# A fused SwiGLU trunk: VectorE's low parts of weights in the order of use, both weight sums ahead of them, output blocks behind a unit's sums

## The chip, the cores and the metric

The kernel runs on one core of one Trainium2 chip. The metric is the device time of one execution in microseconds (us), of which the median of the runs is given. Matrix products run on TensorE (PE in the profile), which accumulates into PSUM banks of 128x512 float32. VectorE (DVE) and ScalarE (ACT) work on tiles of 128 partitions, GpSimd (POOL) and SyncE (SP) issue DMA transfers. Each engine works through its own queue in the order in which the instructions were put there, and waits at the head of the queue for what that instruction needs.

## The reference, cut to what matters

A trunk of two layers on 256 positions (two tiles of 128 rows) of width 2048, all in float32. Layer 0 has a gated mixer and layer 1 a sparse attention; the change touches neither. Behind each mixer come the feed-forward and a gated embedding:

```
D_MODEL, SEQ, PLE_DIM, FFN_DIM = 2048, 256, 256, 5632

def swiglu(h, w_in, w_out):
    g, u = jnp.split(h @ w_in, 2, axis=-1)
    return (jax.nn.silu(g) * u) @ w_out

def ple_add(x, p_i, norm_g, w_proj, w_gate):
    gate = jax.nn.sigmoid(rmsnorm(x, norm_g) @ w_gate)
    return x + (p_i @ w_proj) * gate

for i in range(DEPTH):
    x = x + mixer(rmsnorm(x, norm_mix[i]))
    x = x + swiglu(rmsnorm(x, norm_ffn[i]), ffn_w_in[i], ffn_w_out[i])
    x = ple_add(x, p[i], norm_ple[i], ple_w[i], ple_gate[i])
```

## The kernel before, in words

**Split products.** A float32 product is made of three matmuls in the format fp32r. Both factors are split into a high and a low part, and `mm3` (L155 to L157) sums high x high, high x low and low x high into one bank. The activations are split once. A weight block is split when it comes in (`split`, L148 and L149): ScalarE copies `raw` into the high part, rounding it, and VectorE subtracts that from `raw` for the low part. So each weight block asks for a load, a copy on ScalarE, a subtraction on VectorE and then its matmuls.

**Rings.** `wraw` loads a block of 128x2048 (1 MB) on SP's queue into one of three `raw` buffers, in the order of the blocks. A buffer can be loaded again when its last reader on ScalarE and VectorE is done. The pairs of high and low parts come from `wpair`: a ring of three (`wh` with `wl`), and from part 1 of the feed-forward on of four, in which the fourth lies in a tile called `w4` that holds both parts. A high part can be written again when TensorE has done the last matmul that reads it.

**A unit.** The first product of the feed-forward runs in 11 units `c` of 512 columns of `g` and 512 of `u` (`ffn_unit`, which calls `block_unit`). A unit has eight blocks, one for each two of the 16 tiles of the depth of 2048, and each holds four pieces of 128x512 weights. In an ordinary block all four pieces are used for both row tiles, 8 products of three matmuls. In a block of `pairs7` seven products do, in the manner of Strassen's and Winograd's: VectorE forms four sums of weight pieces in three operations, `t13` (L560, two pieces of 512 in one) and `t24` (L562, then L563, which reads the first half of `t24`):

```
nc.vector.tensor_tensor(t13, r[:, 1:3], r[:, 0:1].to_broadcast([P, 2, NC]), ALU.subtract)
nc.vector.tensor_tensor(t24[:, 0], r[:, 2], t13[:, 0], ALU.add)
nc.vector.tensor_tensor(t24[:, 1], r[:, 3], t24[:, 0], ALU.subtract)
```

The pieces of `raw` that are used as they are (1536 of 2048 columns) are split into one pair of high and low parts, then `t13` and `t24` (1024 columns each) into the halves of the next pair. So a block of seven products takes two pairs of the ring, and VectorE works for it in three sums and three low parts. Unit 0 has three such blocks of eight, units 1, 2 and 3 have four, five and six, and all later units six; the last block of each unit is an ordinary one. The products go into seven banks `p1` to `p7`. In the embedding stage two units of the gate product run through the same `block_unit` with three blocks of seven products each (`PLE_PAIRS`).

**The end of a unit.** `ffn_unit` puts the banks together. ScalarE copies `p1` (L598), VectorE adds `p6`, `p7`, `p2`, `p4`, `p5` and `p3` (`add` at L590, and L605), ScalarE takes two SiLUs (L602 and L604), and VectorE forms the products `up` (L606 and L608). TensorE transposes `up` (`mid_T`), ScalarE and VectorE split that into `aT0` or `aT1`.

**Output jobs.** The second product is cut into parts of one or two units, and each part into four jobs `out_job` of 512 output columns. Behind each unit two of the jobs of earlier parts run (banks `fo`, weight blocks from `in_ffn_w_out`, also through `wraw`, `wpair` and `split`). Each job's sums go to DRAM by a GpSimd DMA that accumulates (`xd<-part`). So between two units' blocks stand four output blocks of 128x2048 (two in the units where a part holds one unit).

**What sets the order.** The program text is not the order on the engines. A scheduler takes the next instruction for each engine among those whose inputs it expects to be ready. What is written under `issue_after(x)` is put behind `x` in the queue of `x`'s engine, without a semaphore; work on other engines isn't touched by it. Before the change none of the work of a unit has such an order, so the sums, low parts and copies stand where the scheduler put them. Layer 0's feed-forward runs from some 286 to 1025 us and layer 1's from some 1405 to 2110. In profile rows, `wl` and `w` (for `w4`) are weight parts, `t` the weight sums `t13` and `t24`, `p` a bank of a unit, `exh`, `exl`, `hF0h`, `hF1h` and the like the split activations.

Of the kernel before, what the change touches and what calls it, by code (L numbers as in the profile page):

```python
# [11 lines left out]
AF = mybir.ActivationFunctionType  # L12
ALU = mybir.AluOpType
# [83 lines left out]
def trunk_kernel(ctx: ExitStack, tc: tile.TileContext, a: dict, out: bass.AP):  # L97
# [40 lines left out]
    def gain(which, k):  # L138
        c = PK_GAIN + which * KD + k
        return pk[:, c:c + 1]  # L140

    def f32v(t):
        return t.bitcast(F32)

    def split(hi, lo, src, scale=None):

        if scale is None:
            nc.scalar.activation(hi, src, AF.Copy)  # L148
            nc.vector.tensor_tensor(lo, src, f32v(hi), ALU.subtract)  # L149
        else:  # L150
            nc.scalar.activation(hi, src, AF.Copy, scale=scale)
            nc.vector.scalar_tensor_tensor(lo, src, scale, f32v(hi), op0=ALU.mult, op1=ALU.subtract)

# [371 lines left out]
    def block_unit(c, forms, win, pairs, early=()):  # L525
# [22 lines left out]
        for at_, j in enumerate(order):  # L548
# [7 lines left out]
            if j in pairs7:  # L556
# [5 lines left out]
                nc.vector.tensor_tensor(t24[:, 0], r[:, 2], t13[:, 0], ALU.add)  # L562
                nc.vector.tensor_tensor(t24[:, 1], r[:, 3], t24[:, 0], ALU.subtract)  # L563
                split(wh[:, NC:], wl[:, NC:], raw[:, NC:])
                prod(1, j, plain(ka, 0), wh, wl, 1, j == last[1])
# [3 lines left out]
                for i, t in enumerate((t13, t24)):  # L569
                    split(wh[:, 2 * i * NC:2 * (i + 1) * NC], wl[:, 2 * i * NC:2 * (i + 1) * NC],  # L570
                          t.rearrange("p s n -> p (s n)"))
                prod(6, j, s2, wh, wl, 2, j == last[6])
# [3 lines left out]
            else:  # L576
                split(wh, wl, raw)
                for b, slots in ((2, (1, 3)), (4, (1, 3)), (5, (0, 2)), (3, (0, 2))):
# [10 lines left out]
    def add(o, p, i):  # L589
        nc.vector.tensor_tensor(o, p, i, ALU.add)  # L590

    def ffn_unit(c, forms, win, rstd, early=()):
# [6 lines left out]
        add(B[:, 0], bank[6], A[:, 0])  # L599
        add(B[:, 1], bank[7], B[:, 0])  # L600
        add(A[:, 0], bank[2], A[:, 0])
# [5 lines left out]
        add(B[:, 0], bank[3], B[:, 0])  # L607
        nc.vector.scalar_tensor_tensor(B[:, 0], B[:, 0], rs[:, 0:1], A[:, 0], op0=ALU.mult, op1=ALU.mult)  # L608
        return B
# [625 lines left out]
```

## Time and profile before

| | us |
|---|---|
| median of 3 runs (lowest, highest) | 2206.74 (2206.36, 2208.51) |
| the profiled execution | 2208.47 |
| its span on the core | 2206.8 |
| VectorE busy in low parts of 128x2048 and other sizes straight from `raw` (375 instructions) | 655.9 |
| VectorE busy in low parts of weight sums (202) | 243.3 |
| VectorE busy in the first weight sum, L560 (129) | 156.9 |
| ScalarE busy in the copies of `raw` (391) | 565.5 |

Read from it: VectorE's busy time holds mostly low parts and weight sums. The profile gives of a group of instructions the mean duration and the idle time of the engine ahead of them, with the engine that ended it. A matmul's row on the time line gives its start and how long it took from start to end; since matmuls overlap, the distance of two starts is what one costs. A row `x2` stands for two instructions.

### The profile page before, as it was taken

Reading aid. Unit: us, or ns where it says so; the run is one execution under the profiler, and the core shown is the slowest. Engines: PE = TensorE matmul, PEld = TensorE weight load, DVE = VectorE, ACT = ScalarE, POOL = GpSimd, SP = SyncE. Lnnn points to the kernel's source line nnn. Section 1 sums busy time; section 2 is a strip of 40 time slices with the busy share of each in tenths; the row PEclk is TensorE's granted clock in tenths of the full one; section 3 lists DMA queues with packets and bytes.
Section 4 is the critical chain, followed back from the end, with each engine's and each line's share of the span. In section 5 each row is a group of like instructions: output and inputs, shape, how many; then the busy total and the mean of one; then the engine's idle time right before and its main releaser. Section 6 shows DMA issues by size and latency. Waiting matters only on the chain.

```text
span 2206.8 us, 26808 instructions
## 1 busy us (share of the span) xinstructions
PE 2188.2 (99%) x10054; PEld 1814.3 (82%) x10054; DVE 1855.8 (84%) x2232; ACT 1351.2 (61%) x1694; POOL 78.3 (4%) x82
## 2 busy tenths in 40 slices
PE   8999999999999999999999999999999999999998
PEld 7888878878888888888888998888888888888887
DVE  5566679999999999878887888799999999999685
ACT  7555556656656565566677877556665565665563
POOL 0000000000000000000000000000000000000000
PEclk9999999999999999999999999999999999999999
DMA  8566555766666776764576455557667667666754
GB/s 314 190 194 228 194 201 191 226 229 224 207 209 218 229 228 210 254 208 171 177 257 201 139 168 194 178 201 238 204 199 234 224 219 234 219 221 211 247 177 153
DMA packets 132430, 464.68 MB, mean 211 GB/s; under 512 B 10811, under 2 KB 13243, under 8 KB 131884
## 3 DMA queue, kind: packets, MB, share of 16 engines
q1 hardware_dynamic: 117596, 431.14, 55.8%
q0 software_dynamic: 13264, 29.63, 7.2%
q10 hardware_dynamic: 1440, 2.20, 0.3%
q8 instruction: 79, 1.29, 0.2%
q14 instruction: 51, 0.42, 0.1%
HBM read 435.63 MB, written 28.38 MB: 210 GB/s over the span
## 4 chain that ended last, share of the span: by engine, by line
PE 89%; DVE 6%; ACT 2%; DMA 2%; issue 1%; SPq 0%; DVEq 0%; ACTq 0%
PE p L156 13%; PE p L157 13%; PE p L155 13%; PE fo L155 7%; PE fo L157 7%; PE fo L156 7%; DVE wl L149 2%; PE v L155 1%; PE v L156 1%; PE v L157 1%; PE ao L157 1%; PE bo L155 1%; PE bo L156 1%; PE bo L157 1%; PE ao L155 1%
## 5 line engine op out<-in xcount | busy, mean ns | idle before, releaser
L149 DVE TENSOR_TENSOR wl<-raw,wh 128x2048 fp32r<-128x2048 f32 (+3 forms) x375 | 655.9, 1753 | 178.0 <-ACT wh L148 177.5
L148 ACT ACTIVATE wh<-raw 128x2048 fp32r<-128x2048 f32 (+3 forms) x391 | 565.5, 1450 | 335.8 <-PE p L157 95.5
L148 ACT ACTIVATE wh<-t 128x1024 fp32r<-128x1024 f32 x202 | 211.8, 1059 | 163.7 <-DVE t L563 73.4
L149 DVE TENSOR_TENSOR wl<-t,wh 128x1024 fp32r<-128x1024 f32 x202 | 243.3, 1218 | 43.4 <-ACT wh L148 43.2
L156 PE MATMUL p<-wl,exh 128*128 128x512 f32 x443 | 174.1, 394 | 0.1
L157 PE MATMUL p<-wh,exl 128*128 128x512 f32 x443 | 172.7, 390 | 0.0
L155 PE MATMUL p<-wh,exh 128*128 128x512 f32 x443 | 168.4, 390 | 0.7 <-ACT wh L148 0.7
L560 DVE TENSOR_TENSOR t<-raw 128x1024 f32<-128x1024 f32 x129 | 156.9, 1216 | 2.4 <-DMA raw<-in_ple_gate 2.4
L156 PE MATMUL p<-wl,hF1h 128*128 128x512 f32 x310 | 121.2, 391 | 0.9 <-DVE wl L149 0.9
L148 ACT ACTIVATE w<-raw 128x1536 fp32r<-128x1536 f32 (+1 forms) x58 | 98.2, 1694 | 37.8 <-DMA raw<-in_ffn_w_in 15.3
L156 PE MATMUL p<-wl,hF0h 128*128 128x512 f32 x310 | 121.1, 391 | 0.3 <-DVE wl L149 0.3
L155 PE MATMUL p<-wh,hF0h 128*128 128x512 f32 x310 | 119.9, 390 | 0.4 <-ACT wh L148 0.4
L157 PE MATMUL p<-wh,hF0l 128*128 128x512 f32 x310 | 120.3, 390 | 0.0
L157 PE MATMUL p<-wh,hF1l 128*128 128x512 f32 x310 | 120.2, 390 | 0.0
L155 PE MATMUL p<-wh,hF1h 128*128 128x512 f32 x310 | 119.8, 390 | 0.0
L149 DVE TENSOR_TENSOR w<-raw,w 128x1536 fp32r<-128x1536 f32 (+1 forms) x58 | 116.4, 2007 | 0.6 <-ACT w L148 0.4
L155 PE MATMUL fo<-wh,aT0h 128*128 128x512 f32 x280 | 109.7, 392 | 0.3 <-DVE gt L590 0.3
L155 PE MATMUL fo<-wh,aT1h 128*128 128x512 f32 x280 | 109.7, 392 | 0.3 <-DVE gt L590 0.3
L157 PE MATMUL fo<-wh,aT0l 128*128 128x512 f32 x280 | 109.8, 392 | 0.0
L157 PE MATMUL fo<-wh,aT1l 128*128 128x512 f32 x280 | 109.8, 392 | 0.0
L156 PE MATMUL fo<-wl,aT0h 128*128 128x512 f32 x280 | 109.1, 389 | 0.0
L156 PE MATMUL fo<-wl,aT1h 128*128 128x512 f32 x280 | 109.0, 389 | 0.0
(345 smaller groups left out, 5129.0 us busy)
## 6 DMA issues: line engine op xcount, KB each, us to landing
raw<-in_ffn_w_in SPq DMA_DIRECT2D x176, 1024.0 KB, 4.8
raw<-in_ffn_w_out SPq DMA_DIRECT2D x88, 1024.0 KB, 6.0
raw<-in_ple_gate SPq DMA_DIRECT2D x32, 1024.0 KB, 4.8
raw<-in_a_w_in SPq DMA_DIRECT2D x63, 512.0 KB, 3.6
xd<-part POOLq DMA_DIRECT2D x40, 512.0 KB, 6.7
raw<-in_a_w_out SPq DMA_DIRECT2D x32, 512.0 KB, 4.2
raw<-in_b_w_out SPq DMA_DIRECT2D x32, 512.0 KB, 3.9
raw<-in_kv_w SPq DMA_DIRECT2D x24, 512.0 KB, 4.3
```

The costliest lines, as they stand in the source:

```text
L148: nc.scalar.activation(hi, src, AF.Copy)
L149: nc.vector.tensor_tensor(lo, src, f32v(hi), ALU.subtract)
L155: nc.tensor.matmul(ps, lh, rh, start=start, stop=False)
L156: nc.tensor.matmul(ps, lh, rl, start=False, stop=False)
L157: nc.tensor.matmul(ps, ll, rh, start=False, stop=stop)
L560: nc.vector.tensor_tensor(t13, r[:, 1:3], r[:, 0:1].to_broadcast([P, 2, NC]), ALU.subtract)
```

## The change

The low parts get an order on VectorE. `split` now returns the instruction of the low part, and `split_behind` issues a split behind others. In `block_unit` each low part is put behind the one before it in the program (`cur["low"]`), and the low parts of `t13` and `t24` also behind the last weight sum of their block (`last_sum`). In the blocks of other products that run on the wide ring (the output blocks, the embedding's weights) the low part is put behind the one before in the same way. At the end of `ffn_unit` the list `ahead` is filled: the next low part is put behind the sum with `p7` (`first`), and the one after that behind the last product (`end`). Only the low parts on VectorE are put in order; the copies on ScalarE remain with the scheduler. The calculation, the instructions and their number stay as they are; the lines of `split`, `add` and the sums have new numbers (L560, L562 and L563 become L574, L576 and L577, L590 and L605 become L605 and L620, L155 to L157 become L164 to L166).

```
@@ -146,10 +146,19 @@
 
         if scale is None:
             nc.scalar.activation(hi, src, AF.Copy)
-            nc.vector.tensor_tensor(lo, src, f32v(hi), ALU.subtract)
-        else:
-            nc.scalar.activation(hi, src, AF.Copy, scale=scale)
-            nc.vector.scalar_tensor_tensor(lo, src, scale, f32v(hi), op0=ALU.mult, op1=ALU.subtract)
+            return nc.vector.tensor_tensor(lo, src, f32v(hi), ALU.subtract)
+        nc.scalar.activation(hi, src, AF.Copy, scale=scale)
+        return nc.vector.scalar_tensor_tensor(lo, src, scale, f32v(hi), op0=ALU.mult, op1=ALU.subtract)
+
+    ahead = []
+
+    def split_behind(hi, lo, src, *others):
+
+
+        with ExitStack() as behind:
+            for ins in (ahead.pop(0) if ahead else []) + [i for i in others if i is not None]:
+                behind.enter_context(tc.issue_after(ins.ins))
+            return split(hi, lo, src)
 
     def mm3(ps, lh, ll, rh, rl, start, stop):
         nc.tensor.matmul(ps, lh, rh, start=start, stop=False)
@@ -165,6 +174,8 @@
 
     def open_stream(wide):
         marks.clear()
+        ahead.clear()
+        cur["low"] = None
         cur["sb"] = es = ExitStack()
         cur["kt"] = 2 * KT if wide else KT
         cur["nblk"] = cur["nw"] = 0
@@ -238,6 +249,9 @@
                 for j in range(kt):
                     f = slice(j * n, (j + 1) * n)
                     split(wh[:, f], wl[:, f], raw[:, f], gain(gains[0], gains[1] + j))
+                return wh, wl
+            if cur["third"] is not None and parts == 1 and kt == cur["kt"]:
+                cur["low"] = split_behind(wh, wl, raw, cur["low"])
                 return wh, wl
             for i in range(parts):
                 f = slice(i * kt * n // parts, (i + 1) * kt * n // parts)
@@ -560,21 +574,22 @@
                 nc.vector.tensor_tensor(t13, r[:, 1:3], r[:, 0:1].to_broadcast([P, 2, NC]), ALU.subtract)
                 t24 = tp.tile([P, 2, NC], F32, tag="t2", name="t24")
                 nc.vector.tensor_tensor(t24[:, 0], r[:, 2], t13[:, 0], ALU.add)
-                nc.vector.tensor_tensor(t24[:, 1], r[:, 3], t24[:, 0], ALU.subtract)
-                split(wh[:, NC:], wl[:, NC:], raw[:, NC:])
+                last_sum = nc.vector.tensor_tensor(t24[:, 1], r[:, 3], t24[:, 0], ALU.subtract)
+                cur["low"] = split_behind(wh[:, NC:], wl[:, NC:], raw[:, NC:], cur["low"])
                 prod(1, j, plain(ka, 0), wh, wl, 1, j == last[1])
                 prod(2, j, plain(kb, 0), wh, wl, 3, j == last[2])
                 prod(3, j, s4, wh, wl, 2, j == last[3])
                 wh, wl = wpair()
                 for i, t in enumerate((t13, t24)):
-                    split(wh[:, 2 * i * NC:2 * (i + 1) * NC], wl[:, 2 * i * NC:2 * (i + 1) * NC],
-                          t.rearrange("p s n -> p (s n)"))
+                    f = slice(2 * i * NC, 2 * (i + 1) * NC)
+                    cur["low"] = split_behind(wh[:, f], wl[:, f], t.rearrange("p s n -> p (s n)"),
+                                              cur["low"], last_sum)
                 prod(6, j, s2, wh, wl, 2, j == last[6])
                 prod(7, j, s3, wh, wl, 1, j == last[7])
                 prod(4, j, plain(kb, 1), wh, wl, 3, j == last[4])
                 prod(5, j, plain(ka, 1), wh, wl, 0, j == last[5])
             else:
-                split(wh, wl, raw)
+                cur["low"] = split_behind(wh, wl, raw, cur["low"])
                 for b, slots in ((2, (1, 3)), (4, (1, 3)), (5, (0, 2)), (3, (0, 2))):
                     for i, s in enumerate(slots):
                         if b == 3:
@@ -587,7 +602,7 @@
         return bank
 
     def add(o, p, i):
-        nc.vector.tensor_tensor(o, p, i, ALU.add)
+        return nc.vector.tensor_tensor(o, p, i, ALU.add)
 
     def ffn_unit(c, forms, win, rstd, early=()):
 
@@ -597,7 +612,7 @@
         B = tp.tile([P, TT, NC], F32, tag="t1", name="up")
         nc.scalar.activation(A[:, 0], bank[1], AF.Copy)
         add(B[:, 0], bank[6], A[:, 0])
-        add(B[:, 1], bank[7], B[:, 0])
+        first = add(B[:, 1], bank[7], B[:, 0])
         add(A[:, 0], bank[2], A[:, 0])
         nc.scalar.activation(A[:, 0], A[:, 0], AF.Silu, scale=rs[:, 0:1])
         add(A[:, 1], bank[4], B[:, 1])
@@ -605,7 +620,8 @@
         nc.vector.tensor_tensor(B, bank[5].unsqueeze(1).to_broadcast([P, TT, NC]), B, ALU.add)
         nc.vector.scalar_tensor_tensor(B[:, 1], B[:, 1], rs[:, 1:2], A[:, 1], op0=ALU.mult, op1=ALU.mult)
         add(B[:, 0], bank[3], B[:, 0])
-        nc.vector.scalar_tensor_tensor(B[:, 0], B[:, 0], rs[:, 0:1], A[:, 0], op0=ALU.mult, op1=ALU.mult)
+        end = nc.vector.scalar_tensor_tensor(B[:, 0], B[:, 0], rs[:, 0:1], A[:, 0], op0=ALU.mult, op1=ALU.mult)
+        ahead[:] = [[first], [end]]
         return B
 
     def ffn(layer, hT, ss, which, which_next):
```

Three places show what it moves. The first is VectorE's queue at the end of a steady unit (layer 0's unit 4). `raw_4552` is its last block of seven products, with the sums `t13_4556` and `t24_4558` that go into `w4_4572`; `raw_4589` is its last block, an ordinary one, and `raw_4648` the first output block behind the unit. Before:

```order
L149 TENSOR_TENSOR wl_4535<-t24_4520,wh_4534 128x1024
L149 TENSOR_TENSOR w4_4572<-t13_4556,w4_4572 128x1024
L562 TENSOR_TENSOR t24_4558<-raw_4552,t13_4556 128x512
L149 TENSOR_TENSOR wl_4592<-raw_4589,wh_4591 128x2048
L563 TENSOR_TENSOR t24_4558<-raw_4552,t24_4558 128x512
L149 TENSOR_TENSOR wl_4651<-raw_4648,wh_4650 128x2048
L149 TENSOR_TENSOR w4_4572<-t24_4558,w4_4572 128x1024
L590 TENSOR_TENSOR up_4620<-p6_4356,gt_4619 128x512
L590 TENSOR_TENSOR up_4620<-p7_4360,up_4620 128x512
L590 TENSOR_TENSOR gt_4619<-p2_4342,gt_4619 128x512
```

In the program of the change the same place reads:

```order
L576 TENSOR_TENSOR t24_4558<-raw_4552,t13_4556 128x512
L577 TENSOR_TENSOR t24_4558<-raw_4552,t24_4558 128x512
L149 TENSOR_TENSOR w4_4572<-t13_4556,w4_4572 128x1024
L149 TENSOR_TENSOR w4_4572<-t24_4558,w4_4572 128x1024
L149 TENSOR_TENSOR wl_4592<-raw_4589,wh_4591 128x2048
L605 TENSOR_TENSOR up_4620<-p6_4356,gt_4619 128x512
L605 TENSOR_TENSOR up_4620<-p7_4360,up_4620 128x512
L605 TENSOR_TENSOR gt_4619<-p2_4342,gt_4619 128x512
L149 TENSOR_TENSOR wl_4651<-raw_4648,wh_4650 128x2048
```

The last weight sum moves ahead of both low parts of `w4_4572`, the low part from `t24_4558` moves ahead of `wl_4592`, and the output block's `wl_4651` moves behind three of the unit's sums.

The second place is ScalarE's queue there, with the copies that these low parts need. Before:

```order
L148 ACTIVATE w4_4572<-t13_4556 128x1024
L148 ACTIVATE wh_4591<-raw_4589 128x2048
L148 ACTIVATE wh_4650<-raw_4648 128x2048
L598 ACTIVATE gt_4619<-p1_4338 128x512
L148 ACTIVATE w4_4572<-t24_4558 128x1024
L148 ACTIVATE wh_4680<-raw_4678 128x2048
L602 ACTIVATE gt_4619<-gt_4619,rstd_2404 128x512
L604 ACTIVATE gt_4619<-gt_4619,rstd_2404 128x512
```

In the program of the change:

```order
L148 ACTIVATE w4_4572<-t13_4556 128x1024
L148 ACTIVATE wh_4591<-raw_4589 128x2048
L148 ACTIVATE wh_4650<-raw_4648 128x2048
L148 ACTIVATE w4_4572<-t24_4558 128x1024
L613 ACTIVATE gt_4619<-p1_4338 128x512
L148 ACTIVATE wh_4680<-raw_4678 128x2048
L617 ACTIVATE gt_4619<-gt_4619,rstd_2404 128x512
L148 ACTIVATE w4_4716<-raw_4714 128x2048
L619 ACTIVATE gt_4619<-gt_4619,rstd_2404 128x512
```

The copy of `t24_4558` comes ahead of the copy of the bank `p1`, but still behind the copy of the output block, `wh_4650`; the second SiLU (L604 before, L619 now) comes behind the copy `w4_4716` of the third output block. On TensorE the rows of this place in the program of the change are these; the last matmul that reads `wh_4534`, whose buffer `wh_4650` gets, stands 18 matmuls ahead of the first row here:

```order
L164 MATMUL p2_4342<-wh_4591,hF0h_1591 128x512
L164 MATMUL p5_4368<-wh_4591,hF0h_1591 128x512
L165 MATMUL p6_4356<-w4_4572,exh_1593 128x512
L166 MATMUL p6_4356<-w4_4572,exl_1594 128x512
L165 MATMUL p4_4364<-w4_4572,hF0h_1591 128x512
L166 MATMUL p4_4364<-w4_4572,hF0l_1592 128x512
L164 MATMUL p4_4364<-wh_4591,hF0h_1591 128x512
L164 MATMUL p3_4346<-wh_4591,exh_1593 128x512
L165 MATMUL p2_4342<-wl_4592,hF0h_1591 128x512
```

The first use of the low part of `t24_4558` is the third row (low x high from `w4_4572` into `p6`), and the first use of `wl_4592` the ninth; before, `wl_4592` was read ahead of that.

The third place is VectorE's queue in the middle of layer 0's unit 2. Before:

```order
L149 TENSOR_TENSOR wl_3141<-t13_3124,wh_3140 128x1024
L563 TENSOR_TENSOR t24_3126<-raw_3121,t24_3126 128x512
L149 TENSOR_TENSOR wl_3161<-raw_3158,wh_3160 128x2048
L149 TENSOR_TENSOR wl_3141<-t24_3126,wh_3140 128x1024
L560 TENSOR_TENSOR t13_3192<-raw_3188 128x1024
L149 TENSOR_TENSOR wl_3191<-raw_3188,wh_3190 128x1536
L562 TENSOR_TENSOR t24_3194<-raw_3188,t13_3192 128x512
L149 TENSOR_TENSOR w4_3208<-t13_3192,w4_3208 128x1024
```

In the program of the change:

```order
L577 TENSOR_TENSOR t24_3126<-raw_3121,t24_3126 128x512
L149 TENSOR_TENSOR wl_3141<-t13_3124,wh_3140 128x1024
L574 TENSOR_TENSOR t13_3192<-raw_3188 128x1024
L149 TENSOR_TENSOR wl_3141<-t24_3126,wh_3140 128x1024
L149 TENSOR_TENSOR wl_3161<-raw_3158,wh_3160 128x2048
L576 TENSOR_TENSOR t24_3194<-raw_3188,t13_3192 128x512
L149 TENSOR_TENSOR wl_3191<-raw_3188,wh_3190 128x1536
L577 TENSOR_TENSOR t24_3194<-raw_3188,t24_3194 128x512
```

The first sum of the next block, `t13_3192` from `raw_3188`, stands ahead of the low part of `t24_3126` and of `wl_3161`, where it stood behind both.

More of the change, by code (lines that the diff above doesn't have):

```diff
@@ L148, in split, with split_behind @@
             nc.scalar.activation(hi, src, AF.Copy)
[L149 to L152, printed above, removed]
+            return nc.vector.tensor_tensor(lo, src, f32v(hi), ALU.subtract)
+        nc.scalar.activation(hi, src, AF.Copy, scale=scale)
+        return nc.vector.scalar_tensor_tensor(lo, src, scale, f32v(hi), op0=ALU.mult, op1=ALU.subtract)
+    ahead = []
+    def split_behind(hi, lo, src, *others):
+        with ExitStack() as behind:
+            for ins in (ahead.pop(0) if ahead else []) + [i for i in others if i is not None]:
+                behind.enter_context(tc.issue_after(ins.ins))
+            return split(hi, lo, src)
     def mm3(ps, lh, ll, rh, rl, start, stop):
@@ L167, in open_stream @@
         marks.clear()
+        ahead.clear()
+        cur["low"] = None
         cur["sb"] = es = ExitStack()
@@ L240, in wblock @@
                     split(wh[:, f], wl[:, f], raw[:, f], gain(gains[0], gains[1] + j))
+                return wh, wl
+            if cur["third"] is not None and parts == 1 and kt == cur["kt"]:
+                cur["low"] = split_behind(wh, wl, raw, cur["low"])
                 return wh, wl
@@ L562, in block_unit @@
                 nc.vector.tensor_tensor(t24[:, 0], r[:, 2], t13[:, 0], ALU.add)
-                nc.vector.tensor_tensor(t24[:, 1], r[:, 3], t24[:, 0], ALU.subtract)
-                split(wh[:, NC:], wl[:, NC:], raw[:, NC:])
+                last_sum = nc.vector.tensor_tensor(t24[:, 1], r[:, 3], t24[:, 0], ALU.subtract)
+                cur["low"] = split_behind(wh[:, NC:], wl[:, NC:], raw[:, NC:], cur["low"])
                 prod(1, j, plain(ka, 0), wh, wl, 1, j == last[1])
@@ L569, in block_unit @@
                 for i, t in enumerate((t13, t24)):
-                    split(wh[:, 2 * i * NC:2 * (i + 1) * NC], wl[:, 2 * i * NC:2 * (i + 1) * NC],
-                          t.rearrange("p s n -> p (s n)"))
+                    f = slice(2 * i * NC, 2 * (i + 1) * NC)
+                    cur["low"] = split_behind(wh[:, f], wl[:, f], t.rearrange("p s n -> p (s n)"),
+                                              cur["low"], last_sum)
                 prod(6, j, s2, wh, wl, 2, j == last[6])
@@ L576, in block_unit @@
             else:
-                split(wh, wl, raw)
+                cur["low"] = split_behind(wh, wl, raw, cur["low"])
                 for b, slots in ((2, (1, 3)), (4, (1, 3)), (5, (0, 2)), (3, (0, 2))):
@@ L589, in add @@
     def add(o, p, i):
-        nc.vector.tensor_tensor(o, p, i, ALU.add)
+        return nc.vector.tensor_tensor(o, p, i, ALU.add)
     def ffn_unit(c, forms, win, rstd, early=()):
@@ L599, in ffn_unit @@
         add(B[:, 0], bank[6], A[:, 0])
-        add(B[:, 1], bank[7], B[:, 0])
+        first = add(B[:, 1], bank[7], B[:, 0])
         add(A[:, 0], bank[2], A[:, 0])
@@ L607, in ffn_unit @@
         add(B[:, 0], bank[3], B[:, 0])
-        nc.vector.scalar_tensor_tensor(B[:, 0], B[:, 0], rs[:, 0:1], A[:, 0], op0=ALU.mult, op1=ALU.mult)
+        end = nc.vector.scalar_tensor_tensor(B[:, 0], B[:, 0], rs[:, 0:1], A[:, 0], op0=ALU.mult, op1=ALU.mult)
+        ahead[:] = [[first], [end]]
         return B
```

## The prediction

> **What bounds the kernel now.** I read four views: the page's busy times and slices, who TensorE waits for, the time lines of three engines at one place in the middle, and the chain of waits at two early places.
>
> ```profile
> span 2206.8 us, 26808 instructions
> ...
> PE 2188.2 (99%) x10054; PEld 1814.3 (82%) x10054; DVE 1855.8 (84%) x2232; ACT 1351.2 (61%) x1694; POOL 78.3 (4%) x82
> ...
> 550.00:612.00 62.00, 62.00 (x278) 50.94 (x277) 57.63 (x53) 37.72 (x33) 2.14 (x2) 1.00 0.67 220
> ```
>
> TensorE is busy 99% of the span. The last row is one whole unit in the middle of layer 0's feed-forward: TensorE 62.00 of 62 us, VectorE 57.63, so VectorE has some 4 us in hand per unit, ScalarE 24. Who TensorE waits for, in 330 to 490 us and then in 1410 to 1610:
>
> ```profile
> PE p L156 <- DVE w L149: 1.0, 1, 1.0
> PE fo L155 <- DVE gt L590: 0.3, 1, 0.3
> PE p L155 <- ACT wh L148: 0.3, 1, 0.3
> PE p L156 <- DVE wl L149: 0.3, 1, 0.3
> ...
> PE p L156 <- DVE wl L149: 0.9, 3, 0.4
> PE p L156 <- DVE w L149: 0.7, 1, 0.7
> PE fo L155 <- DVE gt L590: 0.3, 1, 0.3
> ```
>
> Asked of 490 to 1025 and of 1610 to 2110 the same view names no wait at all. So the reordering can win in the first four units of each layer alone: 1.9 us of idle in four waits, and 1.9 in five. A wait costs a little more than its idle:
>
> ```profile
> 415.33 1.22 DVE L149 TENSOR_TENSOR w<-t,w 128x1024 fp32r<-128x1024 f32 x1
> ...
> 415.17 0.39 PE L157 MATMUL p<-w,exl 128*128 128x512 f32 x1
> 416.61 0.50 PE L156 MATMUL p<-w,exh 128*128 128x512 f32 x1 [1.04 <-DVE w L149]
> 416.95 0.40 PE L157 MATMUL p<-w,exl 128*128 128x512 f32 x1
> ```
>
> The low part ends at 416.55 and TensorE starts 0.06 later. From 415.17 to 416.61 are 1.44 us where a matmul in a row takes 0.227 (worked out below), and the next takes 0.34: 1.21 + 0.11 lost for 1.04 idle, 0.28 more. All nine waits are worth 3.8 + 9 x 0.28 = 6.3 us, the most that the change can win.
>
> **The change part by part.** No instruction is added or removed; costs are those of order alone. VectorE's low parts and the last weight sum of a pair are pinned, and what stands at the head of VectorE's queue now holds up everything behind it.
>
> *The steady units (4 to 10 of both layers).* At a unit's end the order shown above changes: the low part of the last pair's later sums (`w4_4572` from `t24_4558`) now comes ahead of the low part of the unit's last block (`wl_4592`). On ScalarE the copy that it needs still stands behind the copy of the first output block (`wh_4650`). Before:
>
> ```profile
> 590.98 0.62 PE L157 MATMUL p<-wh,hF0l 128*128 128x512 f32 x2
> 597.11 0.39 PE L157 MATMUL p<-wh,hF0l 128*128 128x512 f32 x1
> ...
> 591.64 1.92 ACT L148 ACTIVATE wh<-raw 128x2048 fp32r<-128x2048 f32 x1 [0.86 <-PE p L157]
> 593.47 0.58 ACT L598 ACTIVATE gt<-p 128x512 f32<-128x512 f32 x1
> 594.70 1.06 ACT L148 ACTIVATE w<-t 128x1024 fp32r<-128x1024 f32 x1 [0.65 <-DVE t L563]
> ...
> 588.90 1.22 DVE L149 TENSOR_TENSOR wl<-t,wh 128x1024 fp32r<-128x1024 f32 x1
> 590.04 1.22 DVE L149 TENSOR_TENSOR w<-t,w 128x1024 fp32r<-128x1024 f32 x1
> ...
> 591.78 2.29 DVE L149 TENSOR_TENSOR wl<-raw,wh 128x2048 fp32r<-128x2048 f32 x1
> 593.98 0.69 DVE L563 TENSOR_TENSOR t<-raw,t 128x512 f32<-128x512 f32 x1
> 594.58 2.29 DVE L149 TENSOR_TENSOR wl<-raw,wh 128x2048 fp32r<-128x2048 f32 x1
> ```
>
> From 590.98 to 597.11 are 27 matmuls: 0.227 each. The second of the first row, at 591.21, is the last that reads the buffer which `wh_4650` gets; ScalarE starts that copy 0.43 later, at 591.64, on TensorE's word. Its next operation starts 1.83 later (593.47). After the change this is the copy of the later sums, 1.06: done at 594.53. Here VectorE waits: a low part of 1024 at 594.56 (0.03 as from 593.98 + 0.69 to 594.70), the next start 1.14 behind it (588.90 to 590.04), the low part of 2048 2.29, TensorE 0.06 later: 594.56 + 1.14 + 2.29 + 0.06 = 598.05. In the new TensorE order the first matmul that reads this low part is the 26th after 591.21, due at 597.11. So TensorE waits 0.94 and loses 0.11 on restart: **1.05 us**. The low part of the later sums itself, due 20 matmuls on at 595.75, ends at 595.78: just in time. It was harmless before because VectorE took `wl_4592` first (done at 594.07) and TensorE read the sums last. Everything runs through TensorE's own buffer release, so it comes back in each unit, and no lead of VectorE helps: 14 x 1.05 = **+14.7 us**. What stands behind the waiting low part are the unit's sums and the output blocks' low parts. They keep up: from TensorE's restart R the matmuls that end bank 2 take 1.0, its sum can start at R + 1.45, `wl_4651` behind it ends 0.60 + 2.29 later, at R + 4.34, wanted at R + 4.87 (21 matmuls). VectorE then is 1.4 us later at the next unit's first sum than before, which its 4 us in hand pay. Bounds of this term: nothing, if the copy of the sums slips ahead, and 3 us more per unit, if a load is late (both are rivals).
>
> *The early units (0 to 3).* VectorE sets the pace there. Two places count in each layer. In unit 2 the next pair's first sum, with its load, now stands ahead of two low parts:
>
> ```profile
> 391.38 2.29 DVE L149 TENSOR_TENSOR wl<-raw,wh 128x2048 fp32r<-128x2048 f32 x1 [1.62 <-ACT wh L148]
> 393.59 1.22 DVE L149 TENSOR_TENSOR wl<-t,wh 128x1024 fp32r<-128x1024 f32 x1
> 394.72 1.22 DVE L560 TENSOR_TENSOR t<-raw 128x1024 f32<-128x1024 f32 x1
> ...
> 384.64 9.96 DMA raw<-in_ffn_w_in
> 394.60 0.02 issue
> 394.70 1.50 ACT wh L148
> ...
> 394.91 0.45 PE L156 MATMUL p<-wl,exh 128*128 128x512 f32 x1
> ```
>
> The load lands at 394.60; its buffer's release (384.64) does not move, so neither does this. VectorE now stands idle until then, takes the sum (1.13) and then the low part that TensorE wants at 394.91: ready at 394.65 + 1.13 + 1.22 + 0.06 = 397.06, a wait of 2.15 + 0.11 = **2.2 us**. In unit 3 the same happens once more:
>
> ```profile
> 439.56 7.48 DMA raw<-in_ffn_w_in
> 447.59 0.39 PE L156 MATMUL p<-wl,exh 128*128 128x512 f32 x1
> ```
>
> Load at 447.04, ScalarE's copy of that block (1.50) and of the sums (1.06), the low part 1.22 and 0.06: 450.9 against 447.59 is 3.3. The weight sum that frees this load's buffer now comes one low part (1.14) earlier, so 2.2 to 3.3; I take 2.5. Against 4.7 us per layer stand the old waits, 6.3 / 2 = 3.1, which the sums' place ahead of the low parts takes away. **+1.6 per layer, +3.2 us**; from -3.1 per layer (no new wait) to +4.7 (no old one goes).
>
> *The embedding stage.* Its units have three sum pairs of eight and no copy of sums behind an output block's. Before, TensorE was busy 59.88 of 60 us there:
>
> ```profile
> 1030.00:1090.00 60.00, 59.88 (x279) 49.15 (x279) 55.09 (x83) 39.14 (x61) 0.59 (x1) 1.00 0.48 164
> ```
>
> At most 0.1 us to win, 5 us of VectorE's idle to hide in: 0.
>
> Sum: 14.7 + 3.2 = 17.9 us. The profiled execution took 2208.5 (span 2206.8 and 1.7 around it), so 2226.4; the median of the runs, 2206.7, lies 1.7 lower: **2225 us**.
>
> **The rivals.**
> *Faster.* No wait at the unit's end: if release to low part takes under 5.90 us (26 matmuls) instead of 6.84, nothing is lost from unit 4 on, and if the loads of units 2 and 3 come sooner too, the old waits are all won back: 2206.7 - 6.3 = 2200. For it: all nine waits are on exactly the operations that are pinned. Against: the 6.84 are five measured durations, and the copies' order stands in the program.
> *No change.* As before at the unit's end, the early units as worked out: 2206.7 + 3.2 = 2210.
> *Slower still: the SiLU product behind a load.* ScalarE's second SiLU now stands behind the copy of the third output block, whose load is issued when `wl_4592` ends.
>
> ```profile
> 601.66 0.71 ACT L604 ACTIVATE gt<-gt,rstd 128x512 f32<-128x512 f32 x1
> 603.12 1.92 ACT L148 ACTIVATE w<-raw 128x2048 fp32r<-128x2048 f32 x1 [0.75 <-DMA raw<-in_ffn_w_out]
> raw<-in_ffn_w_out SPq DMA_DIRECT2D x88, 1024.0 KB, 6.0
> raw<-in_ple_gate SPq DMA_DIRECT2D x32, 1024.0 KB, 4.8
> ```
>
> The transposes want the product at R + 8.7 (38 matmuls). Copy 1.92, SiLU 0.71, product 0.74 leave the load about 5.3 us. The median of these loads is 6.0, but two of the four of a unit are issued 0.6 us apart; alone, 4.8 as the gate's. After the change the buffers come free 4 us and more apart, so I count on 4.8; at 6.0 it would be 0.7 late, 14 x 0.7 = 10, 2235. If it took 8.4 (issued by 594.7, at work at 603.1), each unit lost 3 us more: 2225 + 42 = 2267.
> *The clock.*
>
> ```profile
> 2200.00:2207.00 7.00, 1.12 (x5) 0.58 (x4) 2.06 (x6) 0.69 (x1) 0.00 (x0) 0.92 0.19 75
> ```
>
> The granted clock (0.92 of 1) falls only here, once TensorE has run out of work; in all windows above it is 1.00, the one with the 1.04 us wait included. If each new wait cost what this row lost, 0.08 x 7 = 0.56 us, 14 made 8: 2233. The Trainium skill ("TensorE: Matmul & The Clock Gate", "A second HAM failure mode: psum-queue depth-cycling") says that frequent short idles between groups of matmuls can swing the clock between half and full. By its window of 3.4 us at half speed an estimate is 1.7 us per unit, 24 in all, 2249; the trace does not agree so far.
>
> **How the numbers follow.** The forecast 0.65 (2216 to 2235, a load of 6.0 included), late loads 0.10, the clock 0.03, no change 0.13, faster 0.09. The range of 2205 to 2245 leaves out the won-back case and the late loads. Faster by over 0.2% (4.4 us, about what a measurement of this kernel can tell from no change) 0.09, within 0.14 (2210 sits near its edge), slower 0.77.
>
> **What would show it.** In the middle windows: TensorE waiting for `wl L149` once per unit with some 0.8 us idle, VectorE waiting 2 us or more for ScalarE's `wh` or `w` just ahead, a unit of 63.4 instead of 62.35 us. In 384 to 400: VectorE idle until the load of 394.6. Wrong would be: a middle window that still has TensorE at 62.00 of 62, waits of `fo` or the transposes for ScalarE's SiLU, or a granted clock under 1.00.

## The result, and the profile after

| | before | after the change |
|---|---|---|
| median of 4 runs, us | 2207.05 | 2233.11 |
| lowest and highest, us | 2206.36, 2208.51 | 2231.55, 2233.99 |
| ratio, 95% interval | | 1.0117 [1.0101, 1.0133] |
| the profiled execution, us | 2208.47 | 2233.99 |

The kernel is 26 us slower (1.2%); the forecast was 18 slower, with 2205 to 2245 as the range. The first rows are the page's, then who TensorE waits for (us in all, times, longest) in 490 to 1035 us and in 1620 to 2140, then one unit in the middle by engine:

```profile
span 2232.3 us, 26892 instructions
...
PE 2198.9 (99%) x10054; PEld 1810.3 (81%) x10054; DVE 1871.3 (84%) x2232; ACT 1347.8 (60%) x1694; POOL 78.8 (4%) x82
...
PE p L165 <- DVE wl L149: 3.8, 7, 0.6
PE mT L389 <- DVE up L621: 0.5, 1, 0.5
PE mT L389 <- DVE up L623: 0.2, 1, 0.2
...
PE p L165 <- DVE wl L149: 3.8, 7, 0.6
PE xT L340 <- DVE x_sb L380: 2.6, 3, 1.9
PE mT L389 <- DVE up L621: 0.4, 1, 0.4
...
550.00:612.00 62.00, 60.92 (x267) 48.94 (x266) 56.67 (x52) 35.76 (x31) 2.14 (x2) 1.00 0.69 221
```

(The 84 instructions that the page counts more than before are semaphore instructions.) Before, no wait was named in these stretches. Now there are seven waits for `wl` in each layer, one in each unit from 4 on, and in the unit of the last row TensorE works 60.92 of 62 us: it waits 0.54 for `wl` at 602.39 and 0.54 for the transposes' input (`mT`) at 611.90. The granted clock is 1.00 there as before: what is lost is time, not clock.

This is the end of layer 0's unit 5, on ScalarE, on VectorE and on TensorE (start, duration, and in brackets the idle time ahead with what ended it). It is the place that the part ahead of the prediction calls unit 4: counted from unit 0 by the units' SiLUs, unit 4 ended at 539 us before the change and unit 5 at 601. The steady units have the same order, so nothing in the argument hangs on it.

```profile
596.01 1.93 ACT L148 ACTIVATE wh<-raw 128x2048 fp32r<-128x2048 f32 x1 [0.90 <-PE p L166]
597.83 1.05 ACT L148 ACTIVATE w<-t 128x1024 fp32r<-128x1024 f32 x1
...
595.43 0.69 DVE L577 TENSOR_TENSOR t<-raw,t 128x512 f32<-128x512 f32 x1
596.04 1.22 DVE L149 TENSOR_TENSOR w<-t,w 128x1024 fp32r<-128x1024 f32 x1
598.91 1.23 DVE L149 TENSOR_TENSOR w<-t,w 128x1024 fp32r<-128x1024 f32 x1 [1.65 <-ACT w L148]
600.05 2.28 DVE L149 TENSOR_TENSOR wl<-raw,wh 128x2048 fp32r<-128x2048 f32 x1
...
604.47 2.28 DVE L149 TENSOR_TENSOR wl<-raw,wh 128x2048 fp32r<-128x2048 f32 x1
...
600.20 0.49 PE L165 MATMUL p<-w,exh 128*128 128x512 f32 x1
600.53 0.39 PE L166 MATMUL p<-w,exl 128*128 128x512 f32 x1
...
601.46 0.40 PE L164 MATMUL p<-wh,exh 128*128 128x512 f32 x1
602.39 0.51 PE L165 MATMUL p<-wl,hF0h 128*128 128x512 f32 x1 [0.54 <-DVE wl L149]
602.74 0.40 PE L166 MATMUL p<-wh,hF0l 128*128 128x512 f32 x1
```

It is the chain of the prediction, link by link. The last weight sum is done at 596.12, but its copy starts at 597.83, behind the output block's copy that TensorE's release started at 596.01. VectorE stands idle for 1.65 us (the forecast looked for 2 or more), then takes the low part of the sums and only then the one that TensorE waits for. From the start of the output block's copy to the matmul are 602.39 - 596.01 = 6.38 us; forecast were 598.05 - 591.64 = 6.41.

To see where the time comes in, take the same matmul in both traces: its start after the change less its start before is the lag. For the last matmul into the first bank of the last output job behind layer 0's unit 10 the two rows, before and after, are

```profile
933.09 0.39 PE L157 MATMUL fo<-wh,aT0l 128*128 128x512 f32 x1
...
945.92 0.39 PE L166 MATMUL fo<-wh,aT0l 128*128 128x512 f32 x1
```

The lag is 12.83 us there. What each stage adds to it, in us, for the change and for the experiments below:

| | units 0-3, layer 0 | units 4-10 | to the end of unit 0, layer 1 | units 1-3, layer 1 | units 4-10 | rest | sum |
|---|---|---|---|---|---|---|---|
| the change | 3.0 | 9.9 | -1.2 | 1.9 | 9.1 | 2.8 | 25.5 |
| pin_last | 0.8 | 7.0 | -1.5 | 0.7 | 6.9 | 0.0 | 13.9 |
| pin_last_act | -0.4 | 2.5 | -1.5 | 1.1 | 2.5 | 0.0 | 4.3 |
| act_sums_first | 1.2 | 2.8 | -1.0 | 2.5 | 2.0 | 0.1 | 7.6 |
| free_last | 0.9 | 2.5 | -1.1 | 3.0 | 2.4 | 0.0 | 7.7 |
| no_ahead | -0.2 | 8.1 | -1.5 | 0.7 | 7.9 | 0.0 | 15.0 |
| ahead_only | 3.5 | 5.1 | -1.3 | 6.8 | 4.9 | 0.0 | 19.1 |
| no_last_sum | 8.6 | 7.7 | 0.4 | 8.6 | 7.7 | 3.7 | 36.6 |
| no_ahead_act | 0.5 | 1.9 | -1.6 | 0.7 | 1.8 | 0.0 | 3.3 |
| before_act | -0.1 | 2.6 | -1.2 | 0.7 | 2.5 | 0.1 | 4.7 |
| three_units | 0.4 | 0.0 | -1.2 | 0.1 | -0.1 | 0.0 | -0.8 |
| sums_early | -1.6 | -0.1 | -1.7 | 2.5 | -0.1 | 0.3 | -0.7 |

Each row compares one profiled execution with one, and these lie up to 2.1 us from their medians (sums_early 2207.84 against 2209.94), so differences of a us or two between sums say little. Differences in the text are of unrounded values. The column between the layers is about -1.3 in all kernels but one. In every kernel the lag falls by 0.4 to 1.3 us between 1076 and 1408 us, where layer 1's mixer runs, which none of them changes: most likely that belongs to the profiled execution of before, which was 1.4 us above the median.

### The profile page after: what moved, and what is told of

The parts are those of the page before. It is cut to its first block, busy times and chain, and to the rows that moved or that the text cites. A ratio compares the mean times of both kernels' runs of the same rounds, so it can differ in the third digit from the quotient of the medians.

```text
span 2232.3 us, 26892 instructions
## 1 busy us (share of the span) xinstructions
PE 2198.9 (99%) x10054; PEld 1810.3 (81%) x10054; DVE 1871.3 (84%) x2232; ACT 1347.8 (60%) x1694; POOL 78.8 (4%) x82
## 4 chain that ended last, share of the span: by engine, by line
PE 81%; DVE 8%; DMA 4%; issue 4%; ACT 4%; SPq 0%; DVEq 0%; ACTq 0%
PE p L165 12%; PE p L166 12%; PE p L164 11%; PE fo L166 6%; PE fo L165 6%; PE fo L164 6%; DVE wl L149 4%; ACT wh L148 2%; DMA raw<-in_ffn_w_out 2%; DMA raw<-in_ffn_w_in 1%; PE ao L166 1%; PE u L164 1%; PE ao L164 1%; PE ao L165 1%; PE u L165 1%
## 5 line engine op out<-in xcount | busy, mean ns | idle before, releaser
L164 PE MATMUL p<-wh,exh 128*128 128x512 f32 x443 | 172.8, 392 | 3.9 <-ACT wh L148 3.9
L166 PE MATMUL p<-wh,exl 128*128 128x512 f32 x443 | 172.5, 390 | 0.0
L574 DVE TENSOR_TENSOR t<-raw 128x1024 f32<-128x1024 f32 x129 | 157.5, 1221 | 11.1 <-DMA raw<-in_ffn_w_in 8.2
L166 PE MATMUL p<-wh,hF1l 128*128 128x512 f32 x310 | 120.9, 390 | 0.0
L166 PE MATMUL p<-wh,hF0l 128*128 128x512 f32 x310 | 120.9, 390 | 0.0
L164 PE MATMUL p<-wh,hF0h 128*128 128x512 f32 x310 | 119.4, 391 | 0.3 <-ACT wh L148 0.3
L164 PE MATMUL p<-wh,hF1h 128*128 128x512 f32 x310 | 119.1, 390 | 0.0
L164 PE MATMUL fo<-wh,aT1h 128*128 128x512 f32 x280 | 110.1, 393 | 0.0
L164 PE MATMUL fo<-wh,aT0h 128*128 128x512 f32 x280 | 110.0, 393 | 0.0
L166 PE MATMUL fo<-wh,aT0l 128*128 128x512 f32 x280 | 109.6, 391 | 0.0
L166 PE MATMUL fo<-wh,aT1l 128*128 128x512 f32 x280 | 109.6, 391 | 0.0
```

The costliest lines, as they stand in the source:

```text
L164: nc.tensor.matmul(ps, lh, rh, start=start, stop=False)
L166: nc.tensor.matmul(ps, ll, rh, start=False, stop=stop)
```

## The experiments

Theory A: in the steady units (4 to 10) the loss is the copy's order, as above. Theory B: it comes from the edges `ahead`, which put the output blocks' low parts behind the unit's sums. Theory C: from the last weight sum ahead of both low parts.

**pin_last: the inversion alone.** On the kernel before, from unit 4 on. The output block's low part gets an edge too, so that the scheduler doesn't move it ahead:

```
# block_unit, behind the splits of t13 and t24
+ cur["later"] = cur["lo"]                    # the low part of t24
# block_unit, the ordinary block
+ if j == NPAIR - 1 and c >= 4:
+     behind.enter_context(tc.issue_after(cur["later"].ins))
  split(wh, wl, raw)
+ cur["after"] = [cur["lo"]]                  # (last block, c >= 4)
# wblock, the next block
+ for ins in cur.pop("after", ()):
+     behind.enter_context(tc.issue_after(ins.ins))
```

> The kernel before (about 2207 us) with two edges on VectorE alone, in units 4 to 10 of both layers: the low part of the unit's last block stands behind the low part of the later sums of the block ahead of it, and the first output block's low part behind that one. ScalarE's copy of those sums still stands behind the copy of the first output block. Theory A (the steady units lose because that low part waits for a ScalarE copy that stands behind a copy which waits for TensorE to release a buffer): one wait of 0.5 to 0.9 us of TensorE per unit for wl at the unit's last block, 14 x (0.82 to 1.05) = 11.5 to 14.7 us, 2218 to 2222 us. Theory B (the loss of the change comes from the output blocks' low parts behind the unit's sums, which free the load buffers late) and theory C (it comes from the last weight sum ahead of both low parts, which makes low parts arrive just in time): 2207 us, no wait there.

Measured: 2221.63 us against 2207.41, ratio 1.0064 [1.0049, 1.0079]: 14.2 us. Who TensorE waits for, in 490 to 1035 and in 1620 to 2140:

```profile
PE p L156 <- DVE wl L149: 3.9, 7, 0.6
...
PE p L156 <- DVE wl L149: 3.8, 7, 0.6
```

The same fourteen waits for `wl` as in the change, and no other in these stretches. The two edges cost 1.0 us per unit; forecast for this wait was 1.05. B and C, which said 2207, don't explain it.

**pin_last_act: and the copy in the same order.** As above, with the output block's copy behind the copy of `t24`:

```
+ cur["later"], cur["sums"] = cur["lo"], cur["hi"]
+ cur["after"] = [cur["lo"], cur["sums"]]
```

> The same two edges on VectorE, and one on ScalarE: the copy of the first output block stands behind the copy of the later sums, so that these no longer wait for TensorE's release. Theory A: the wait at the unit's end goes, 2206 to 2209 us. If VectorE's order alone made the loss, whatever ScalarE does: as the run without this edge, 2218 to 2222 us. Theories B and C: 2207 us, as without the edge.

Measured: 2212.80 us, ratio 1.0024 [1.0014, 1.0034]. In 490 to 1035 and 1620 to 2140 no wait is named any more, so the wait is indeed the copy's; but 5.4 us stay, 0.36 per unit, where A said none. See before_act.

**act_sums_first: the whole change with that edge on ScalarE.**

```
  for i, t in enumerate((t13, t24)):
...
+ cur["sums"] = cur["hi"]
# wblock, wide ring
- cur["low"] = split_behind(wh, wl, raw, cur["low"])
+ cur["low"] = split_behind(wh, wl, raw, cur["low"], cur.pop("sums", None))
```

> The whole change (2233 us) with one edge on ScalarE: the copy of the first output block behind a unit stands behind the copy of the unit's last later sums; VectorE's order stays that of the change. Theory A: the 0.82 us per unit go, 14 x 0.82 = 11.5 us, and up to 1.4 us per unit where the later losses came from the same delay: 2213 to 2222 us, and no wait for wl over 0.3 us at the units' ends. Theories B and C: 2232 to 2234 us.

Measured: 2217.04 us, ratio 1.0044 [1.0028, 1.0061]: 16.1 us won back out of 26, by one edge on another engine. The end of layer 0's unit 6 on ScalarE and VectorE:

```profile
656.71 1.06 ACT L148 ACTIVATE wh<-t 128x1024 fp32r<-128x1024 f32 x1 [1.08 <-DVE t L577]
657.68 0.58 ACT L614 ACTIVATE gt<-p 128x512 f32<-128x512 f32 x1
658.15 1.91 ACT L148 ACTIVATE w<-raw 128x2048 fp32r<-128x2048 f32 x1
...
656.59 2.44 DVE L149 TENSOR_TENSOR wl<-t,wh 128x1024 fp32r<-128x1024 f32 x2
658.95 2.29 DVE L149 TENSOR_TENSOR wl<-raw,wh 128x2048 fp32r<-128x2048 f32 x1
```

ScalarE copies the sums as soon as they are there, and VectorE takes both low parts of the sums in a row (the `x2`) and then the last block's, without idling.

**free_last: VectorE's order undone at this place alone.** The change, with the last block of a unit split without the edge:

```
+ if j == NPAIR - 1:
+     split(wh, wl, raw)
+ else:
      cur["low"] = split_behind(wh, wl, raw, cur["low"])
```

> The whole change (2233.1 us) with the low part of a unit's last block left free; in the program VectorE then takes it ahead of the last weight sum and of both low parts of the sums, as before the change. ScalarE's copies stand as before. Theory A: the wait for the last block's low part goes as it does with the edge on ScalarE, 2215 to 2222 us, unless the later sums' low part, now the last, is wanted early by TensorE: then a wait for w in its place, 2225 us or more.

Measured: 2218.31 us, ratio 1.0048 [1.0032, 1.0064]. In the steady units 2.5 and 2.4 us are left of 9.9 and 9.1, about as much as with the edge on ScalarE (2.8 and 2.0), and no wait for `wl` is named there. So it takes VectorE's order and ScalarE's together to make the wait; either one put right ends it.

**pin_last_more: a longer chain.** pin_last with the first quarter of the last block's low part computed once more ahead of the whole:

```
- split(wh, wl, raw)
+ nc.scalar.activation(wh, raw, AF.Copy)
+ nc.vector.tensor_tensor(wl[:, :NC], raw[:, :NC], f32v(wh[:, :NC]), ALU.subtract)
+ cur["lo"] = nc.vector.tensor_tensor(wl, raw, f32v(wh), ALU.subtract)
```

> The run with two edges on VectorE (2221.6 us), with one more operation of VectorE in the chain: in units 4 to 10 the first quarter (512 columns) of the last block's low part is computed once ahead of the whole of it, 0.60 us more between the later sums' low part and that low part. Theory A (VectorE waits in that chain, and what it does behind the wait reaches TensorE in full): 14 x 0.60 = 8.4 us more, 2230 us, the wait for wl 1.1 us instead of 0.54. If VectorE's lead covered a part of it: less, down to 2222 us.

Measured: 2232.06 us, ratio 1.0111 [1.0093, 1.0129], 10.4 us more than pin_last. VectorE there, and TensorE's waits in 490 to 1035:

```profile
661.23 1.23 DVE L149 TENSOR_TENSOR wl<-t,wh 128x1024 fp32r<-128x1024 f32 x1 [1.95 <-ACT wh L148]
662.38 0.69 DVE L585 TENSOR_TENSOR wl<-raw,wh 128x512 fp32r<-128x512 f32 x1
663.10 2.29 DVE L586 TENSOR_TENSOR wl<-raw,wh 128x2048 fp32r<-128x2048 f32 x1
...
PE p L156 <- DVE wl L586: 8.9, 7, 1.3
```

The added operation takes 663.10 - 662.38 = 0.72 us here, not 0.60, and the wait grows from 3.9 / 7 = 0.56 to 1.27. 14 x 0.72 = 10.1: all of it reaches TensorE.

**no_ahead: the change without the edges at the unit's end.**

```
- ahead[:] = [[first], [end]]
```

> The whole change without the two edges that put the output blocks' low parts behind the unit's sums. In the program the first output block's low part now stands behind one sum instead of three, the second behind four instead of all. Theory A: the wait for wl at the unit's end is ahead of these and stays, 2229 to 2234 us. Theory B: the loss of the steady units goes, 2212 to 2216 us. Theory C: 2233 us.

Measured: 2225.36 us, ratio 1.0079 [1.0064, 1.0094]. The seven waits per layer stay (3.9 and 3.8 us), as A has it. Yet 7.7 us go, which no theory had: by the table, which shows 10.5 between these two traces, 3.2 and 1.2 in units 0 to 3, 1.7 and 1.2 in the steady units, 2.8 at the end.

**ahead_only: these edges alone on the kernel before.**

```
- cur["low"] = split_behind(wh[:, NC:], wl[:, NC:], raw[:, NC:], cur["low"])
+ split(wh[:, NC:], wl[:, NC:], raw[:, NC:])
...
- cur["low"] = split_behind(wh, wl, raw, cur["low"])
+ split(wh, wl, raw)
```

> The kernel before with the two edges at a unit's end alone (first output block's low part behind the sum with p7, the second behind the last product); nothing else is pinned, and VectorE takes the last block's low part ahead of that of the later sums, as before. Theory A (only the copies' order costs): 2207 us. Theory A with a smaller part D (the output blocks' low parts behind the sums free the load buffers late and leave the next unit's first parts and the end of layer 1 late; taking these edges out of the whole change has won 7.7 us): 2209 to 2216 us, with no wait for wl at the units' ends. Theory C (last weight sum ahead of both low parts): 2207 us.

Measured: 2227.50 us, ratio 1.0092 [1.0075, 1.0109]: 20 us, far above what was expected. TensorE's waits in 490 to 1035, one of them, and the first use of the output block's low part behind unit 5 in the change:

```profile
PE fo L165 <- DVE w L149: 1.3, 4, 0.4
PE fo L165 <- DVE wl L149: 1.1, 3, 0.4
...
670.05 0.50 PE L165 MATMUL fo<-w,aT0h 128*128 128x512 f32 x1 [0.33 <-DVE w L149]
...
607.29 0.39 PE L165 MATMUL fo<-wl,aT0h 128*128 128x512 f32 x1
```

Without the order of use the scheduler puts the first output block's low part behind four of the unit's sums, in the change behind three. One more sum is 0.60 us, and in the change this low part ends at 604.47 + 2.28 = 606.75, wanted at 607.29: 0.54 to spare. So here it comes late, by another wait in another place, 0.7 us per unit; units 0 to 3 lose 3.5 and 6.8. The parts don't add up: this wait and that of pin_last would both stand in the change if they added. There TensorE, held up for `wl`, reaches the output block later.

**no_last_sum: the change without the edges from the last weight sum.**

```
- cur["low"], last_sum)
+ cur["low"])
```

> The whole change (2233 us) without the edges from the last weight sum to the low parts; the low parts stay in the order of use. In the program the last weight sum stands between the two low parts. Theory A: the later sums' copy waits for the output block's copy all the same, 2231 to 2235 us, 0.5 us of wait per unit. Theory C, as a part of the whole: the low parts that arrive just in time (some 0.3 us per unit beside the long wait) come earlier, 14 x 0.3 = 4 us, 2228 to 2230 us.

Measured: 2245.64 us, ratio 1.0175 [1.0159, 1.0190], 12.5 us slower than the change, a miss for both theories. The steady units win 2.2 and 1.4 us per layer (as C has it, if less), but units 0 to 3 lose 5.7 and 6.7 more. TensorE's waits in 330 to 490, in the change and here, and VectorE here at the end of unit 3:

```profile
PE p L164 <- ACT wh L148: 1.5, 1, 1.5
PE p L165 <- DVE wl L149: 1.4, 2, 0.9
PE p L165 <- DVE w L149: 0.4, 1, 0.4
...
PE p L165 <- DVE wl L149: 4.2, 5, 1.5
PE p L164 <- ACT wh L148: 0.7, 2, 0.4
PE mT L389 <- DVE up L623: 0.7, 1, 0.7
...
474.91 0.68 DVE L577 TENSOR_TENSOR t<-raw,t 128x512 f32<-128x512 f32 x1
477.46 1.23 DVE L149 TENSOR_TENSOR w<-t,w 128x1024 fp32r<-128x1024 f32 x1 [1.86 <-ACT w L148]
```

In order of use alone, low parts are held up behind copies of sums that come late, as in the last row: the last weight sum ends only at 475.59, its copy on ScalarE starts at 476.38 behind the output block's, and VectorE stands idle for 1.86 us. With the early last sum it takes these low parts without idling there (470.43, in the change). It is the one part of the change that wins something, and what it mends is the order of use. (The longest single wait, 1.5 us at 399.48, is another one: VectorE has idled 2.11 us for a load, as in the change.)

**no_ahead_act: both repairs.** no_ahead with the edge of act_sums_first.

> The change without the two edges at a unit's end and with the edge on ScalarE that puts the output block's copy behind that of the later sums. If the parts add up (2225.4 for the first alone, 16.1 us won by the second alone): 2208 to 2212 us; what is left then is 0.3 us per unit of low parts that arrive just in time. If both repair the same loss, it stays at 2217 us.

Measured: 2212.82 us, ratio 1.0024 [1.0014, 1.0034]. They add up to a good part: 7.7 and 16.1 would make 2209.3. What is left in the steady units (1.9 and 1.8 us) is no more than the edge on ScalarE costs by itself on the kernel before (2.6 and 2.5, next).

**before_act: the edge on ScalarE alone, on the kernel before.**

```
+ cur["after"] = [cur["hi"]]        # behind the splits of t13 and t24; used in wblock as in pin_last
```

> The kernel before with the edge on ScalarE alone: the first output block's copy behind that of the later sums, VectorE's order free. Theory A says nothing of a gain here, since VectorE does not wait in this chain in the kernel before: 2206 to 2209 us. If ScalarE's order alone made the difference of 9 to 16 us that the edge made in the other two runs: well under 2207 us.

Measured: 2213.35 us, ratio 1.0026 [1.0016, 1.0037]: 5.6 us slower. So the edge has a price of its own, 0.36 us per steady unit, as large as what stayed in pin_last_act. One such place, the first output block behind layer 0's unit 6 (start, duration):

```profile
664.50 0.39 PE L157 MATMUL p<-wh,exl 128*128 128x512 f32 x1
664.96 0.47 PE L155 MATMUL fo<-w,aT0h 128*128 128x512 f32 x1
665.27 0.40 PE L156 MATMUL fo<-w,aT0h 128*128 128x512 f32 x1
```

0.46 and 0.31 from start to start instead of 0.227. The output block's low part stands ahead of the unit's sums here, as in the kernel before, and the view names two waits of `fo` for such a sum (`fo <- DVE gt`, 1.4 us each, at 476.88 and 1600.22); that the sums also make the lost tenths in the steady units isn't shown. Nor is it shown that the two 0.36 have one cause: in pin_last_act the lost tenths stand at low parts of the unit's last blocks.

**three_units and sums_early: looking for a gain in the early units.** The first has the order of use and the last sums first in units 0 to 2 alone, without `ahead`; the second, on the kernel before, only the last sum ahead of both low parts, in units 0 to 3:

```
# three_units, on the change
+ cur["pin"] = pairs is FFN_PAIRS and c < 3      # edges only where this holds, no ahead
# sums_early, on the kernel before
+ if pairs is FFN_PAIRS and c < 4:
+     behind.enter_context(tc.issue_after(last_sum.ins))
```

> The pins of the change (order of use, last weight sum) in units 0, 1 and 2 of both layers alone, without the edges at a unit's end; from unit 3 on and in the embedding the order is free as before. In the run without those edges layer 0 was 2.1 us ahead of the kernel before at the end of unit 2 and layer 1 0.1 us: 2204 to 2206 us if that lead lasts, 2207 us or more if unit 3 gives it back.

> The kernel before with the edges from the last weight sum to both low parts of sums, in units 0 to 3 of the feed-forward alone; no order of use, nothing else. Taking these edges out of the whole change cost 12.5 us, most of it in units 0 to 3. If they win by freeing the load buffers earlier, by themselves too: up to 6.3 us (all waits that the kernel before has there), 2201 to 2205 us. If they only mend what the order of use breaks: 2206 to 2209 us.

Measured: 2209.25 us, ratio 1.0007 [0.9997, 1.0016], and 2209.94 us, ratio 1.0010 [1.0001, 1.0020]. Neither wins anything. In sums_early layer 0 gains 1.6 us, and layer 1 gives 2.5 back: in each layer one wait of 2.3 us appears for a unit's sum (`fo <- DVE gt`) in the place of the old ones. No version beat the kernel before.

## Why the prediction came out as it did

The profiled execution came 25.5 us later, not 17.9: by the table the steady units took 19.0 instead of 14.7, the early ones 4.9 instead of 3.2, the end of layer 1 2.8 instead of nothing, and -1.2 lies between the layers.

**The steady units: the wait right in mechanism and size.** The forecast was 1.05 us per unit from one wait. pin_last, which has only this, measured 1.0; act_sums_first and free_last end the wait from either side. The idle time listed is 0.54, where the forecast looked for some 0.8, but idle counts from the end of the matmul before, 0.40 behind its start. By starts, the matmul comes 602.39 - 601.46 - 0.227 = 0.70 late, the one behind it 0.12, and 0.19 were lost in the 25 matmuls from 595.59 to 601.46. Part of that is at the low part of the sums: it ends at 598.91 + 1.23 = 600.14, 0.06 before its matmul, and that matmul and the next lie 0.33 apart. Together they make 1.01.

**The step that was too small is "they keep up".** What stands behind the waiting low part was costed at nothing. The output block's low part does keep up: forecast was to end 4.34 behind the restart, wanted at 4.87; measured are 606.75 - 602.39 = 4.36 and 607.29 - 602.39 = 4.90. But the steady units lost 9.9 + 9.1 = 19.0 us, not 14.7; without the `ahead` edges it is 16.1, without the last sums' edges 15.4. Some three us come with each, where the forecast had none. The lag shows where they stand: inside each of layer 0's seven steady units it grows by 1.12 to 1.19 us (0.97 to 1.03 in pin_last), and between them by 1.8 in all, of which 0.8 lie behind unit 5. Their trace is tenths: low parts that end within 0.1 us of their matmul, and transposes held up for 0.2 to 0.5 us by the SiLU product. From wait to wait a steady unit of layer 0 took 63.5 to 63.6 us, and 64.3 and 63.9 where the transposes waited; the forecast was 63.4.

**The early units: forecast +3.2, measured 3.0 + 1.9 = 4.9.** Here is the first of the two new waits, in unit 2:

```profile
394.21 1.23 DVE L574 TENSOR_TENSOR t<-raw 128x1024 f32<-128x1024 f32 x1 [3.89 <-DMA raw<-in_ffn_w_in]
395.35 1.22 DVE L149 TENSOR_TENSOR wl<-t,wh 128x1024 fp32r<-128x1024 f32 x1
...
396.63 0.50 PE L165 MATMUL p<-wl,exh 128*128 128x512 f32 x1 [0.92 <-DVE wl L149]
```

VectorE does stand idle for the load, 3.89 us, but starts the sum at 394.21, where the load of before landed at 394.60, and TensorE gets there later: the matmul ahead starts at 395.32, so this one was due at 395.55, not at 394.91. It starts 1.08 late instead of 2.15. In unit 3 the wait is 1.5, for ScalarE's copy (`wh`), not 2.5 or so. A wait of 0.5 that the forecast counted from unit 4 on alone stands at the end of unit 3 too, in both layers (at 475.28 and 1606.76). The old waits did not all go (`w` 1.0 before, 0.4 now), so the balance came out near by luck, with errors against each other. no_ahead shows that the early loss (3.2 in layer 0, which is all of it, and 1.2 of 1.9 in layer 1) belongs mostly to the edges at the unit's end, which the forecast had not costed in units 0 to 3 at all.

**The end of layer 1: not forecast.** GpSimd reloads `x` in four pieces, the last two behind the last accumulating writes. Before, then after the change:

```profile
2055.34 0.72 POOL L656 DMA_DIRECT2D x_sb<-xd  x1 [6.71 <-DMA xd<-part]
...
2066.34 0.72 POOL L656 DMA_DIRECT2D x_sb<-xd  x1 [6.83 <-DMA xd<-part]
...
2083.22 0.72 POOL L672 DMA_DIRECT2D x_sb<-xd  x1 [11.90 <-DMA xd<-part]
...
2097.59 0.72 POOL L672 DMA_DIRECT2D x_sb<-xd  x1 [12.54 <-DMA xd<-part]
```

The writes that GpSimd waits for take 11.9 and 12.5 us of idle instead of 6.7 and 6.8, and the last piece starts 2097.59 - 2066.34 = 31.3 us later, where the lag at the end of unit 10 is 22.7 (3.0 + 9.9 - 1.2 + 1.9 + 9.1). TensorE then waits 2.6 us for `x`. Of the kernels that have no long wait here, no_ahead and act_sums_first show 8.2 to 10.8 us of idle at the same two places; no_last_sum, the other one that waits (1.9 us), shows 11.3 and 9.7. So the wait is gone without the `ahead` edges (no_ahead), and also where the copy is put in order (act_sums_first). What makes the writes land late stays open: that it is the output blocks' loads on the same DMA engines was not tried.

**The rivals.** Late loads did show in places. This is the third output block's copy behind unit 5 on ScalarE, in the change:

```profile
608.53 1.92 ACT L148 ACTIVATE w<-raw 128x2048 fp32r<-128x2048 f32 x1 [3.23 <-DMA raw<-in_ffn_w_out]
```

It starts 6.2 us after the low part that frees the buffer (600.05 + 2.28), not 4.8, and the second SiLU stands behind it. By the waits named first it costs the transposes 0.5 and 0.4 us in one unit of each layer, not 0.7 or 3 in each unit. The clock rival fell: with fourteen waits in the steady units PEclk is 1.00 in the window above, and in every window of 40 to 100 us from 330 to 1100 and from 1410 to 2140. The Trainium skill ("TensorE: Matmul & The Clock Gate", "A second HAM failure mode: psum-queue depth-cycling") has frequent short idles swing the clock; one wait of 0.5 us in each unit doesn't do it here.

## What to carry to other kernels

Where low parts are put in the order of use on one engine, look at the order of the copies that feed them on the other: an in-order queue makes a late copy hold up every low part behind it, and the copy may stand behind one that waits for TensorE. To find the price, follow the chain from the last buffer release to the matmul and count the matmuls between; slack on VectorE over the whole unit says nothing about it. And cost each edge of a bundle at every place where it acts: here one part mended what another broke, and a third cost more in the early units and at the end of layer 1, where the forecast had not costed it, than in the steady units.

## What the runs showed of the hardware that was not expected

A low part that ends just in time costs TensorE a tenth of a us that the view of waits doesn't list: the matmul that reads it and the next lie 0.33 us apart (600.20 to 600.53) instead of 0.227, and 0.35 behind a listed wait (602.39 to 602.74). A VectorE operation that writes over the result of a 128x512 operation just ahead of it starts 0.72 us behind that one (pin_last_more, 662.38 to 663.10), as one that reads such a result does (the change, 594.71 to 595.43); operations of that size otherwise follow at 0.60 (before, 600.23 to 600.83).
